# Shifted convolution input: on-chip copies by ScalarE and VectorE, or a trip through device memory

## The chip, the cores and the metric

The kernel runs on one core of a Trainium2 chip. The metric is the device time of one execution in microseconds (us). Before the change the median of 3 runs is 1649.34 us (1648.95 to 1651.52).

## What is computed

One inference step of a small decoder trunk with two layers, for a prompt of 512 tokens and for 8 sample sequences of 4 tokens with a paged cache, in fp32, with a model width of 1024. The first layer has a Conformer convolution module, the second an attention with stick-breaking weights; each is followed by an MLP. The change concerns the prompt's convolution module:

```python
def conformer_conv(h, conv_prev, pw1_w, pw1_b, dw_w, dw_b, ln_g, ln_b, pw2_w):
    a, g = jnp.split(h @ pw1_w + pw1_b, 2, axis=-1)
    u = a * jax.nn.sigmoid(g)
    full = jnp.concatenate([conv_prev, u], axis=1)
    y = lax.conv_general_dilated(full, dw_w[:, None, :], (1,), 'VALID',
                                 dimension_numbers=('NWC', 'WIO', 'NWC'),
                                 feature_group_count=D_MODEL) + dw_b
    y = jax.nn.silu(layer_norm(y, ln_g, ln_b))
    return y @ pw2_w, full[:, -(CONV_WIDTH - 1):]
```

The convolution works on each of the 1024 channels alone, with 31 taps along the tokens. For the prompt `conv_prev` is zero.

## The kernel before

The prompt's activations lie as 8 tiles of 128 channels x 512 tokens. A matrix product in fp32 accuracy is made of three products of fp32r operands, split into a high and a low part (`mm3`, line 326): a weight tile `whi` is cast by ScalarE (line 316), its remainder `wlo` made by VectorE (line 319).

**The projection** (loop from line 783) makes `u` tile by tile, `kt` = 0 to 7, from two weight tiles each. The gate `sg` is an activation on ScalarE (line 866), `u` itself one instruction on VectorE (line 875). The last 30 tokens of `u` are kept in `utail` (line 882). Between these, the sample's own projection and convolution (`sample_pw1`, `sconv`) and the first adaLN matrices of the sample stream (`early`, `ada_group`) are put; `ada_sb` (line 250) is ScalarE's copy of such a result and `adat_B` its transpose on TensorE (line 254).

**The convolution.** Tiles 0 and 2 (`TAPS`) are convolved on VectorE, one instruction for each tap (`conv_taps`, line 690). The six others (`REST`) go to TensorE. There, four copies of 32 channels stand in the four quarters of the partitions, each shifted by one token more than the last, so that one product with a 32-row block of weights adds up four taps: `raw[k][32 j + c, g, t] = u[32 g + c, t + j - 30]`, zero where the token is negative. To make this, `u` is stored to the DRAM tensor `ud` (line 877), whose edges are zeroed once from `zpad` (lines 879 to 881), and read back four times, once for each shift (`conv_load`, lines 700 to 703). All of these transfers go through the queue of GpSimd (`pdma`). The tile `raw` (named `ur`) has two buffers. Tiles 1 and 3 are loaded in the projection; `conv(k)` (line 705) makes the weights `wk` on VectorE (line 707), does its 64 matmuls `cv` (line 713), adds the bias on ScalarE into `y[k]` (line 715), starts the row norm's statistics, and at its end loads the tile after next (line 718). Both engines' work is in order within its queue.

The rest of the kernel is two generators, `sample()` and `prompt()`, taken in turn by costs written in the code (line 1498). The order of the instructions on every engine is set by a planner that simulates a timeline:

```python
    with _tile.TileContext(nc, schedule_with_timeline_sim=True) as tc:
        yoco_step_kernel(tc, *args)
```

`order(ins, after)` (line 333) keeps one instruction behind another in that order without a wait. The two small loads `bias_p` and `ptab` (lines 893, 894) are issued after the last store of `u`.

Of the kernel before, what the change touches and what calls it, by code (L numbers as in the profile page):

```python
# [8 lines left out]
F32 = mybir.dt.float32  # L9
# [8 lines left out]
P = 128  # L18
D = 1024
KT = 8  # L20
T = 512
# [6 lines left out]
CW = 31  # L28
# [83 lines left out]
def yoco_step_kernel(  # L112
# [9 lines left out]
    nc = tc.nc  # L122
# [3 lines left out]
    vec = nc.vector  # L126
    dma = nc.sync.dma_start
    pdma = nc.gpsimd.dma_start

    def pool(stack, name, side=None, **kw):  # L130
        kw.setdefault("bufs", 1)
        return stack.enter_context(tc.tile_pool(name=name, side=side, **kw))
# [6 lines left out]
    dr = pool(ctx, "dr", space=DRAM)  # L139
    done = set()  # L140

    def pm(name="pm"):
        return ps.tile([P, 512], F32, tag="pm", bufs=3, name=name)
# [13 lines left out]
    def tmp(name="tmp"):  # L157
        return pp.tile([P, 512], F32, tag="tmp", bufs=4, name=name)

    def vtiles():  # L160
        return [pp.tile([P, T], F32, tag="v", bufs=KT, name="v") for _ in range(KT)]
# [3 lines left out]
    pl = pool(p1, "p1", "left")  # L165
# [70 lines left out]
    def pcol(row, kt):  # L236
        return prm[:, row, kt : kt + 1]
# [66 lines left out]
    def wstage(src, k, queue=nc.scalar, after=None):  # L304
# [4 lines left out]
            after.append(ins)  # L309
        return st.rearrange("p (k c) -> p k c", k=k)  # L310

    def wsplit(st, c0, cw, wp=wp, after=None, chain=None):
        k = st.shape[1]
        hi = wp.tile([P, k, cw], F32R, tag="whi", bufs=2, name="whi")
        lo = wp.tile([P, k, cw], F32R, tag="wlo", bufs=2, name="wlo")
        ins = nc.scalar.copy(hi, st[:, :, c0 : c0 + cw])  # L316
        if after:
            order(ins, after)
        ins = vec.tensor_tensor(lo, st[:, :, c0 : c0 + cw], hi.bitcast(F32), op=ALU.subtract)  # L319
        if chain is not None:  # L320
            in_turn(chain, ins)
        return hi, lo
# [3 lines left out]
    def mm3(out, whi, wlo, xh, xl, start, stop, after=None):  # L326
        first = mm(out, whi, xh, start=start, stop=False)  # L327
        if after:
            order(first, after)
        mm(out, wlo, xh, start=False, stop=False)  # L330
        latest[:] = [mm(out, whi, xl, start=False, stop=stop)]  # L331

    def order(ins, after):
        tc.add_manual_dep(ins.ins, after.ins.name,
                          mybir.DependencyInfo(mybir.DependencyClass.NoSync, mybir.DependencyReason.DATA), reason="issue order")
        return ins
# [73 lines left out]
    def parts(halves):  # L410
        return (slice(0, 256), slice(256, 512)) if halves else (ALL,)

    def in_turn(chain, ins):
        if chain:
            order(ins, chain[-1])
        chain.append(ins)
# [250 lines left out]
    p0.close()  # L667

    utail = pl.tile([P, KT, CW + 1], F32, name="utail")
    zpad = pl.tile([P, KT, CW + 1], F32, name="zpad")  # L670
    ud = dr.tile([KT, P, T + 32], F32, name="ud")

    s1 = ExitStack()
    sl = pool(s1, "s1", "right")
# [2 lines left out]
    y = vtiles()  # L677
    cnrm = Norm()
    raw = {}


    TAPS = (0, 2)
    REST = [k for k in range(KT) if k not in TAPS]
# [12 lines left out]
    def some_taps(n):  # L696
        for _ in itertools.islice(taps, n):
            pass

    def conv_load(k):  # L700
        raw[k] = pld.tile([P, 4, T + 28], F32, tag="ur", bufs=2, name="ur")
        for j in range(4):
            pdma(raw[k][32 * j : 32 * j + 32], ud[k].rearrange("(g c) t -> c g t", g=4)[:, :, j : j + T + 28])

    def conv(k):
        wk = pld.tile([P, 32, 32], F32, tag="wk", bufs=2, name="wk")
        vec.tensor_tensor(wk, sel4.unsqueeze(1).to_broadcast([P, 32, 32]),
                          wtap[:, k, :].unsqueeze(2).to_broadcast([P, 32, 32]), op=ALU.mult)
        for ts in parts(H_CV and k == KT - 1):
            a = pm("cv")[:, 0 : ts.stop - ts.start]  # L710
            for m in range(8):
                for g in range(4):
                    mm(a[32 * g : 32 * g + 32, :], wk[:, 8 * g + m, :], raw[k][:, g, 4 * m + ts.start : 4 * m + ts.stop],  # L713
                       start=(m == 0), stop=(m == 7), tile_position=(0, 32 * g))
            act(y[k][:, ts], a, AF.Identity, bias=pcol(R_DWB, k))
            cnrm.add(y[k], k, ts)
        if k in REST[:-2]:
            conv_load(REST[REST.index(k) + 2])

    sy = sfm("sy", "sv", 2)  # L720

# [61 lines left out]
    for c in range(4):  # L783
        st = []
        for o in range(2):
            src = conv_pw1_w[0, :, o * D + c * 256 : o * D + c * 256 + 256]
# [13 lines left out]
        if c == 0:  # L800
# [5 lines left out]
            def weights(i, o, after):  # L806
                ws[2 * i + o] = wsplit(st[o], i * P, P, plc if i else wp, after, first_chain)
# [33 lines left out]
            for k in range(KT):  # L841
                t = tmp("ax0")
                nc.scalar.mul(t, ubuf[k], ALPHA)
                axd_dma = pdma(axd[0][k], t)
# [9 lines left out]
        for i in range(2):  # L854
            kt = 2 * c + i
            if c:
                ws = [wsplit(st[o], i * P, P) for o in range(2)]
                accs = [pm("pw1") for _ in range(2)]
                for a, (whi, wlo) in zip(accs, ws):
                    for k in range(KT):  # L860
                        mm3(a, whi[:, k, :], wlo[:, k, :], hhi[k], hlo[k], k == 0, k == KT - 1)
                acc = accs
            else:
                acc = accs[2 * i : 2 * i + 2]
            sg = tmp("sg")
            act(sg, acc[1], AF.Sigmoid, bias=pcol(R_PWB + 1, kt))
            for _ in itertools.islice(early, EIN if c else 0):
                pass
            if kt in TAPS:
                upad[kt] = pld.tile([P, T + CW], F32, tag="upad", bufs=len(TAPS), name="upad")  # L870
                vec.memset(upad[kt][:, 0 : CW - 1], 0.0)
                u = upad[kt][:, CW - 1 : T + CW - 1]
            else:
                u = tmp("u")
            vec.scalar_tensor_tensor(u, acc[0], pcol(R_PWB, kt), sg, op0=ALU.add, op1=ALU.mult)
            if kt not in TAPS:
                u_dma = pdma(ud[kt][:, CW - 1 : T + CW - 1], u)
            if kt == 0:
                pad = order(nc.gpsimd.memset(zpad, 0.0), axd_dma)
                pdma(ud[:, :, 0 : CW - 1].rearrange("k p t -> p k t"), zpad[:, :, 0 : CW - 1])  # L880
                pdma(ud[:, :, T + CW - 1 :].rearrange("k p t -> p k t"), zpad[:, :, 0:2])
            nc.scalar.copy(utail[:, kt, 0 : CW - 1], u[:, T - CW + 1 : T])
            if kt in REST[:2]:
                conv_load(kt)
            some_taps(5)


# [1 line left out]
    bias_p = base.tile([P, 2 * H], F32, name="bias_p")  # L889
    bq = base.tile([P, 8], F32, name="bq")  # L890
    nbq = base.tile([P, 2], F32, name="nbq")
    with tc.issue_after(u_dma.ins):
        pdma(bias_p[:, 0:H], attn_bias.to_broadcast([P, H]))
        pdma(ptab.rearrange("p s g -> p (s g)"), page_table.rearrange("(o s) g -> o (s g)", o=1).to_broadcast([P, NS * NPG]))
    nc.gpsimd.tensor_scalar_mul(bias_p[:, H:], bias_p[:, 0:H], -1.0)
# [646 lines left out]
```

## Time and profile before

| | |
|---|---|
| runs (median, lowest, highest) | 1649.34, 1648.95, 1651.52 us |
| the profiled execution, its own time | 1650.69 us |
| its span, first to last instruction | 1648.9 us |
| busy: TensorE, VectorE, ScalarE, GpSimd | 1553.3, 954.8, 569.4, 181.2 us |
| mean granted clock of TensorE | 0.979 |
| mean DMA rate | 248 GB/s |

The engines are named PE (TensorE matmul), PEld (its weight loads), DVE (VectorE), ACT (ScalarE), POOL (GpSimd) and SP (SyncE); a q behind the name is the engine's sequencer. Times are us from the start of the span. "idle before" is the time that the engine sat idle just before an instruction, with what ended it. The clock is the granted share of TensorE's full speed. `L713` is line 713 of the kernel.

### The profile page before, as it was taken

How to read it: one execution, taken by the hardware profiler on the slowest of the kernel's cores; microseconds unless marked ns; L12 is line 12 of the kernel's file. 1: busy time of each engine (PE TensorE's matmuls, PEld its weight loads, DVE VectorE, ACT ScalarE, POOL GpSimd, SP SyncE). 2: the span in 40 equal slices, each digit the busy share in tenths (PEclk: the TensorE clock that was granted, in tenths of full speed). 3: DMA queues.
4: the chain of work that ended last, by engine and by line, in shares of the span. 5: the costliest groups of instructions: out<-in, count | busy, mean ns of one | idle time of the engine just before them, and what ended most of it. 6: DMA issues, size and time to landing. Idle time of an engine off the chain costs nothing.

```text
span 1648.9 us, 25461 instructions
## 1 busy us (share of the span) xinstructions
PE 1553.3 (94%) x10489; PEld 1088.2 (66%) x10489; DVE 954.8 (58%) x1818; ACT 569.4 (35%) x907; POOL 181.2 (11%) x201
## 2 busy tenths in 40 slices
PE   6999989989999999999899999889889999999995
PEld 4666325656777777777478775557767767566885
DVE  4599545565676655655643448984765434233446
ACT  2322123261332233323332535852362323223342
POOL 1210200000012121110012113021111100000002
PEclk9999999999999999999999999999999999999998
DMA  9898879688667776676889878265546585885311
GB/s 327 279 329 305 230 283 368 246 325 309 225 232 266 272 270 239 224 253 226 343 282 331 281 272 313 96 241 193 193 154 239 185 335 182 352 339 180 96 62 51
DMA packets 152358, 409.24 MB, mean 248 GB/s; under 512 B 8197, under 2 KB 82213, under 8 KB 127651
## 3 DMA queue, kind: packets, MB, share of 16 engines
q1 hardware_dynamic: 50819, 161.86, 26.3%
q0 software_dynamic: 22944, 149.07, 25.2%
q10 hardware_dynamic: 78480, 96.70, 17.6%
q8 instruction: 82, 1.34, 0.3%
q14 instruction: 33, 0.27, 0.0%
HBM read 390.56 MB, written 17.88 MB: 248 GB/s over the span
## 4 chain that ended last, share of the span: by engine, by line
PE 78%; DMA 8%; issue 6%; DVE 5%; ACT 2%; POOL 1%; DVEq 0%; SPq 0%; POOLq 0%; ACTq 0%
PE pd L327 18%; PE pd L331 18%; PE pd L330 17%; PE zt L1071 3%; PE av L1122 3%; PE sd_acc L551 3%; PE cv L713 2%; DMA adaw<-in_ada_w_dram 2%; PE w_acc L578 1%; DMA kraw<-in_cache_k_dram,krow 1%; PE pw L327 1%; PE pw L330 1%; PE pw L331 1%; DMA stage<-in_conv_pw_w_dram 1%; PE ada_A L246 1%
## 5 line engine op out<-in xcount | busy, mean ns | idle before, releaser
L319 DVE TENSOR_TENSOR wlo<-stage,whi 128x1024 fp32r<-128x1024 f32 x184 | 223.1, 1215 | 216.8 <-ACT whi L316 216.4
L327 PE MATMUL pd<-xhi,whi 128*128 128x512 f32 (+1 forms) x832 | 321.4, 388 | 9.6 <-ACT whi L316 5.2
L316 ACT CAST whi<-stage 128x1024 fp32r<-128x1024 f32 x184 | 191.6, 1046 | 400.3 <-PE pd L331 350.6
L330 PE MATMUL pd<-xhi,wlo 128*128 128x512 f32 (+1 forms) x832 | 318.5, 384 | 2.7 <-DVE wlo L319 2.7
L331 PE MATMUL pd<-xlo,whi 128*128 128x512 f32 (+1 forms) x832 | 313.1, 386 | 5.6 <-DVE xlo L460 5.6
L1065 DVE STREAM_TRANSPOSE kt<-kraw 128x512 f32<-128x512 f32 x256 | 164.1, 685 | 138.8 <-DMA kraw<-in_cache_k_dram,krow 92.5
L327 PE MATMUL pd<-h2h,whi 128*128 128x512 f32 (+1 forms) x544 | 206.7, 388 | 1.6 <-DVE v L1240 1.0
L330 PE MATMUL pd<-h2h,wlo 128*128 128x512 f32 (+1 forms) x544 | 205.0, 382 | 0.0
L331 PE MATMUL pd<-h2l,whi 128*128 128x512 f32 (+1 forms) x544 | 205.0, 383 | 0.0
L327 PEld LDWEIGHTS pd<-xhi,whi 128*128 128x128 f32 x832 | 160.7, 193 | 59.7 <-issue 13.7
L331 PEld LDWEIGHTS pd<-xlo,whi 128*128 128x128 f32 x832 | 156.5, 192 | 61.1 <-issue 18.2
L330 PEld LDWEIGHTS pd<-xhi,wlo 128*128 128x128 f32 x832 | 160.9, 193 | 42.1 <-issue 10.8
L1240 DVE SCALAR_TENSOR_TENSOR v<-pd,mod_B,v 128x512 f32<-128x512 f32 x120 | 87.8, 745 | 114.1 <-PE pd L331 113.9
L1043 POOL DMA_INDIRECT kraw<-in_cache_k_dram,krow x64 | 66.3, 1035 | 621.1 <-DVE kt L1065 387.9
L327 PEld LDWEIGHTS pd<-h2h,whi 128*128 128x128 f32 x544 | 101.9, 188 | 34.8 <-issue 10.4
L1215 ACT ACTIVATE relu<-pd 128x512 f32<-128x512 f32 (+1 forms) x68 | 38.9, 572 | 239.7 <-PE pd L331 222.3
L331 PEld LDWEIGHTS pd<-h2l,whi 128*128 128x128 f32 x544 | 101.8, 188 | 28.8 <-issue 9.4
L330 PEld LDWEIGHTS pd<-h2h,wlo 128*128 128x128 f32 x544 | 102.2, 188 | 25.0 <-issue 6.7
L1043 POOL DMA_INDIRECT vt<-in_cache_v_dram,vrow x64 | 70.3, 1098 | 273.4 <-PE av L1122 222.9
L1071 PE MATMUL zt<-kt,qb 128*32 128x128 f32 x2048 | 76.8, 279 | 8.2 <-DVE kt L1065 7.7
L1071 PEld LDWEIGHTS zt<-kt,qb 128*32 128x32 f32 x2048 | 52.8, 110 | 33.2 <-issue 16.4
L368 DVE BATCH_NORM_STATS2 bn<-lnT 128x6 f32<-128x128 f32 x160 | 36.5, 284 | 60.0 <-PE lnT L366 59.8
(300 smaller groups left out, 1987.7 us busy)
## 6 DMA issues: line engine op xcount, KB each, us to landing
sw<-in_mlp_w_dram SPq DMA_DIRECT2D x64, 1024.0 KB
stage<-in_mlp_w_dram ACTq DMA_DIRECT2D x64, 1024.0 KB
adaw<-in_ada_w_dram SPq DMA_DIRECT2D x40, 1024.0 KB
stage<-in_conv_pw_w_dram ACTq DMA_DIRECT2D x10, 1024.0 KB
adaw<-in_ada_w_dram SPq DMA_DIRECT2D x16, 512.0 KB
swkv<-in_w_kv_dram SPq DMA_DIRECT2D x8, 1024.0 KB
stage<-in_w_kv_dram ACTq DMA_DIRECT2D x8, 1024.0 KB
ur<-ud POOLq DMA_DIRECT2D x24, 270.0 KB, 8.0
```

What stands on the lines that cost most here:

```text
L316: ins = nc.scalar.copy(hi, st[:, :, c0 : c0 + cw])
L319: ins = vec.tensor_tensor(lo, st[:, :, c0 : c0 + cw], hi.bitcast(F32), op=ALU.subtract)
L327: first = mm(out, whi, xh, start=start, stop=False)
L330: mm(out, wlo, xh, start=False, stop=False)
L331: latest[:] = [mm(out, whi, xl, start=False, stop=stop)]
L551: mm(acc[32 * g : 32 * g + 32, :], hT[:, kk * 2 + kp, :], blk[:, kp * D + c * 512 : kp * D + c * 512 + 512], start=(kk == 0), stop=(kk == ...
L1043: nc.gpsimd.indirect_dma_start(out=out, out_offset=None, in_=cache.rearrange("g (r e) h d -> (g r) (e h d)", e=2), in_offset=bass.Indirect ...
L1065: ins = vec.transpose(kt[:, 2 * x : 2 * x + 2, :], raw[x].rearrange("p (e c) -> p e c", e=2)[:, :, c0 : c0 + 256])
L1071: behind(mm(zt[u][32 * g : 32 * g + 32, f * P : f * P + P], qb[:, u, hh * 8 + bl].rearrange("p x q -> p (x q)"), kt[:, :, bl * 32 : bl * 3 ...
L1122: behind(mm(av[32 * g : 32 * g + 32, :], wT[u][:, i, e, a, :], vt[:, e * D + u * 512 : e * D + u * 512 + 512], start=(a == 0 and i == 0), ...
L1215: latest_act[:] = [act(r, a, AF.Relu)]
L1240: ins = vec.scalar_tensor_tensor(v[kt][:, ts], a, gt[:, kt, 8:9], v[kt][:, ts], op0=ALU.mult, op1=ALU.add)
```

## The change

`u` of the six `REST` tiles is written into `y[k]` directly. The store to `ud`, the zeroing and the four reads go. `conv_load` clears the edges of `raw` (two memsets on VectorE) and copies 16 blocks of 32 partitions x some 512 tokens, each from one quarter of the partitions into another or the same. For tiles 1 and 3, in the projection, all 16 are on ScalarE, put into the loop five at a time; for the four tiles that are loaded within the convolutions, 8 are on ScalarE and 8 on VectorE. ScalarE's copies are ordered behind the last `whi` cast issued so far. `bias_p` and `ptab` are issued after an earlier transfer.

```diff
+    last_whi = []
+
     def wsplit(st, c0, cw, wp=wp, after=None, chain=None):
...
         ins = nc.scalar.copy(hi, st[:, :, c0 : c0 + cw])
         if after:
             order(ins, after)
+        last_whi[:] = [ins]
...
     utail = pl.tile([P, KT, CW + 1], F32, name="utail")
-    zpad = pl.tile([P, KT, CW + 1], F32, name="zpad")
-    ud = dr.tile([KT, P, T + 32], F32, name="ud")
...
     raw = {}
+    loads = []
...
-    def conv_load(k):
+    def conv_load(k, both):
         raw[k] = pld.tile([P, 4, T + 28], F32, tag="ur", bufs=2, name="ur")
-        for j in range(4):
-            pdma(raw[k][32 * j : 32 * j + 32], ud[k].rearrange("(g c) t -> c g t", g=4)[:, :, j : j + T + 28])
+
+        vec.memset(raw[k][:, :, 0 : CW - 1], 0.0)
+        vec.memset(raw[k][:, :, T + CW - 4 :], 0.0)
+        for g in range(4):
+            for j in range(4):
+                out = raw[k][32 * j : 32 * j + 32, g, CW - 1 - j : min(T + CW - 1 - j, T + 28)]
+                src = y[k][32 * g : 32 * g + 32, 0 : out.shape[-1]]
+                if both and (g + j) % 2:
+                    vec.tensor_copy(out, src)
+                else:
+                    order(nc.scalar.copy(out, src), last_whi[0])
+                    yield
...
         if k in REST[:-2]:
-            conv_load(REST[REST.index(k) + 2])
+            for _ in conv_load(REST[REST.index(k) + 2], True):
+                pass
...
             else:
-                u = tmp("u")
+                u = y[kt]
             vec.scalar_tensor_tensor(u, acc[0], pcol(R_PWB, kt), sg, op0=ALU.add, op1=ALU.mult)
-            if kt not in TAPS:
-                u_dma = pdma(ud[kt][:, CW - 1 : T + CW - 1], u)
-            if kt == 0:
-                pad = order(nc.gpsimd.memset(zpad, 0.0), axd_dma)
-                pdma(ud[:, :, 0 : CW - 1].rearrange("k p t -> p k t"), zpad[:, :, 0 : CW - 1])
-                pdma(ud[:, :, T + CW - 1 :].rearrange("k p t -> p k t"), zpad[:, :, 0:2])
             nc.scalar.copy(utail[:, kt, 0 : CW - 1], u[:, T - CW + 1 : T])
             if kt in REST[:2]:
-                conv_load(kt)
+                loads.append(conv_load(kt, False))
+            for _ in itertools.islice(itertools.chain(*loads), 5 if kt < KT - 1 else 32):
+                pass
             some_taps(5)
...
-    with tc.issue_after(u_dma.ins):
+    with tc.issue_after(axd_dma.ins):
```

## Rows read from the trace of the kernel before

**Rows 1.** The page's first part: busy time, share and instructions of each engine.

```profile
PE 1553.3 (94%) x10489; PEld 1088.2 (66%) x10489; DVE 954.8 (58%) x1818; ACT 569.4 (35%) x907; POOL 181.2 (11%) x201
```

**Rows 2.** Busy time by stretch: us, each engine (instructions), granted clock, DMA share, GB/s.

```profile
65.00:155.00 90.00, 86.54 (x533) 59.26 (x531) 87.42 (x156) 25.23 (x46) 11.44 (x20) 1.00 0.88 294
155.00:248.00 93.00, 83.10 (x643) 31.64 (x635) 49.68 (x148) 17.73 (x30) 10.71 (x20) 0.97 0.82 272
248.00:1649.00 1401.00, 1335.28 (x9061) 965.60 (x9061) 795.04 (x1465) 507.21 (x805) 151.71 (x144) 0.98 0.66 240
85.00:106.00 21.00, 17.62 (x116) 10.64 (x112) 21.00 (x34) 3.93 (x6) 0.56 (x1) 1.00 1.03 345
196.00:208.00 12.00, 7.04 (x58) 2.29 (x54) 6.61 (x23) 1.10 (x2) 3.23 (x6) 0.98 1.01 257
208.00:220.00 12.00, 12.00 (x96) 3.76 (x100) 3.11 (x12) 0.69 (x1) 0.00 (x0) 0.88 0.16 33
```

**Rows 3.** TensorE's waits, 65 to 155 us, then 155 to 250: total, times, longest.

```profile
PE ada_B L246 <- DMA adaw<-in_ada_w_dram: 3.4, 3, 2.2
...
PE cv L713 <- DMA ur<-ud: 5.0, 1, 5.0
PE w_acc L578 <- DMA sw<-in_mlp_w_dram: 3.7, 4, 1.4
```

**Rows 4.** TensorE in order of time around 208 us: start, us, instruction, idle before.

```profile
207.94 5.12 PE L713 MATMUL cv<-ur,wk 128*32 128x512 f32 x32 [4.96 <-DMA ur<-ud]
...
213.57 3.64 PE L713 MATMUL cv<-ur,wk 128*32 128x512 f32 x32
```

**Rows 5.** GpSimd's issues of the reads; the page's DMA issues (KB each, landing).

```profile
81.08 2.19 POOL L703 DMA_DIRECT2D ur<-ud  x4 [5.29 <-DMA ud<-u]
...
194.87 2.18 POOL L703 DMA_DIRECT2D ur<-ud  x4 [11.04 <-PE cv L713]
...
ur<-ud POOLq DMA_DIRECT2D x24, 270.0 KB, 8.0
```

**Rows 6.** TensorE in order of time, the first and last wait for `adaw`.

```profile
98.82 1.06 PE L246 MATMUL ada_B<-adaw,cT 128*32 128x512 f32 x8 [0.20 <-DMA adaw<-in_ada_w_dram]
...
105.85 1.07 PE L246 MATMUL ada_B<-adaw,cT 128*32 128x512 f32 x8 [0.96 <-DMA adaw<-in_ada_w_dram]
```

**Rows 7.** VectorE, then TensorE, in order of time in the projection.

```profile
113.77 1.23 DVE L319 TENSOR_TENSOR wlo<-stage,whi 128x1024 fp32r<-128x1024 f32 x1 [0.81 <-ACT whi L316]
...
122.49 1.21 DVE L319 TENSOR_TENSOR wlo<-stage,whi 128x1024 fp32r<-128x1024 f32 x1
...
124.48 0.39 PE L330 MATMUL pw<-xhi,wlo 128*128 128x512 f32 x1
...
135.37 0.60 PE L254 MATMUL adat_B<-c,ada_sb 128*128 128x128 f32 x4
```

**Rows 8.** Groups of instructions: busy us, mean ns, idle before.

```profile
L1278 ACT CAST xhi<-v 128x512 fp32r<-128x512 f32 x8 | 4.8, 604 | 0.0
...
L715 ACT ACTIVATE v<-cv,prm 128x512 f32<-128x512 f32 x6 | 4.1, 685 | 36.8 <-PE cv L713 36.8
...
L946 DVE COPY qr<-qr 32x1024 f32<-32x1024 f32 x3 | 2.1, 685 | 0.1
...
L980 DVE COPY nka<-kv_sb 32x256 f32<-32x256 f32 x4 | 1.1, 286 | 0.1
...
L707 DVE TENSOR_TENSOR wk<-c,wtap 128x1024 f32<-128x1024 f32 x6 | 7.3, 1220 | 3.8 <-PE cv L713 3.8
```

**Rows 9.** ScalarE in order of time.

```profile
133.99 0.22 ACT L882 COPY utail<-u 128x30 f32<-128x30 f32 x1 [2.46 <-DVE u L875]
134.56 0.59 ACT L250 COPY ada_sb<-ada_B 128x512 f32<-128x512 f32 x1 [0.36 <-DVE sy L745]
135.39 1.05 ACT L316 CAST whi<-stage 128x1024 fp32r<-128x1024 f32 x1 [0.24 <-PE pw L331]
...
181.41 0.42 ACT L910 ACTIVATE shT<-sy 128x256 f32<-128x256 f32 x1 [7.45 <-DVE sy L909]
```

## The prediction, made before the changed kernel ran

> **What bounds the kernel now.** I first read the page's head: TensorE is busy for 94% of the span [rows 1], so time is won only where TensorE waits, and a saving elsewhere is hidden. Next came busy time by stage [rows 2]. The change touches two stages. In the projection (65 to 155 us) TensorE idles 90.00 - 86.54 = 3.5 us, VectorE is busy 87.42 of 90 us, and ScalarE 25.23. In the convolution (155 to 248 us) TensorE idles 93.00 - 83.10 = 9.9 us, with VectorE at 49.68 and ScalarE at 17.73. The waits then name what ended that idle time [rows 3]: 3.4 us are weights `adaw` still on the DMA, in the projection; in the convolution 5.0 us are one wait of `cv` for `ur`, the transfer that the change removes, and 3.7 us are sample weights; the rest is smaller.
>
> The order of time shows that one wait [rows 4]: TensorE starts a convolution at 207.94 us after 4.96 us of waiting, since 203.0. Its four reads were issued at 194.87 [rows 5], when the DMA engines were full (share 1.01 between 196 and 208 us, [rows 2]), and the last landed some 11 us after its issue ended at 197.05, against a median of 8.0. After it the clock is low: 32 matmuls take 5.12 us, the next 32 take 3.64 [rows 4]; between 208 and 220 us the granted clock is 0.88 of the upper level, in the projection it is 1.00 [rows 2].
>
> **The change, part by part.** The sum is made against the profiled execution, 1650.69 us, whose span is 1648.9; the median of the runs shown, 1649.34, is 1.35 us below it. A measurement of this kernel can tell about 0.2%, 3.3 us, from no change.
>
> *Removed: the wait for `ur`.* The four tiles loaded inside the convolutions no longer come by DMA. Gain 5.0 us [rows 3]. With the pause goes the slow clock behind it: 5.12 - 3.64 = 1.5 us [rows 4]. Next in line to be late are the copies themselves, priced below.
>
> *Removed: traffic.* Six stores of 256 KB, 24 reads of 270 KB and 128 KB of zeros go, about 8.3 MB. In the projection, the reads of tile 1, issued at 81.08 [rows 5], compete with the `adaw` blocks that TensorE awaits three times, first at 98.8 and last at 105.9 us [rows 6]. They are 1.1 MB; at the 345 GB/s of that stretch [rows 2] they delay the rest by 3.2 us. But VectorE is busy 21.00 of 21 us there [rows 2]. The low half of a later weight tile, `wlo`, is made at 122.49 and is ready at 123.70, and TensorE wants it at 124.48 [rows 7], 0.8 us of slack; VectorE idles another 0.8 us before the preceding `wlo` [rows 7]. A TensorE that arrives 3.2 us earlier therefore keeps about 1.6 us and waits for VectorE with the rest. I take 1.6; the bounds are 0 and 3.4. By the Trainium skill, DMA: Bandwidth & Descriptors, Queues, rings and completion order, each DMA engine goes round the queues that have work, a packet at a time, so that a queue taken away hands its turns to the others at once. By that rule the `adaw` wait would go whole and its term be 3.4; no row here shows the turns. This is a rival below.
>
> *Added: ScalarE's copies.* 32 for the first two tiles in the projection, then 8 for each of four tiles, 64 in all. No row shows one of 32 partitions; the nearest, a ScalarE cast of 128x512 between on-chip tiles, takes 604 ns [rows 8], and I take it. The lower end is `utail`'s 30 columns at 0.22 us [rows 9], the upper end 685 ns, the eviction of 128x512 with a bias [rows 8]. In the projection five copies follow each `utail` copy, 3.0 us, on an engine that idles 65 of 90 us [rows 2], and TensorE's waits there name `adaw` alone [rows 3], so the weight casts have slack. The tightest place is 133.99: `ada_sb` follows at 134.56 and a `whi` cast at 135.39 [rows 9]. If `ada_sb` falls behind the copies, TensorE's `adat_B` at 135.37 [rows 7] waits about 2.6 us: 133.99 + 0.22 + 3.0 + 0.59 less 135.37 is 2.4, and 0.2 for the handover. The program issues `ada_sb` first, so I take 0 and keep 2.6 as an end.
>
> *Added: VectorE's copies.* 8 for each of four tiles, 32 in all. The nearest rows are copies between partition quarters: 32x256 in 286 ns and 32x1024 in 685 [rows 8], so 512 columns take 286 + 256 x 399/768 = 419 ns; the ends are those two rows. That is 3.4 us a tile, 13.4 in all. The two memsets of a tile, 120 columns and 4, I put at 0.3 us together, what the copy of 256 columns takes [rows 8].
>
> *What covers them.* Tile k+2 is copied after convolution k ends, while convolution k+1 runs: 64 matmuls, two times 3.64 us [rows 4], 7.2 us. On ScalarE the copies are 8 x 0.604 behind the eviction (0.69), 5.5 us; on VectorE 3.4 + 0.3 behind the 1.2 us of `wk`, 4.9 us [rows 8]. Both are below 7.2, so I cost them at 0. Without that cover a tile costs up to 5.5 us of TensorE wait. What queues behind them on VectorE is the sample's layer norm, whose `shT` ScalarE makes at 181.41 after 7.45 us of waiting [rows 9], and the statistics of the row norm.
>
> *Moved.* The queue of GpSimd loses 32 issues, and the two small loads for `bias_p` and `ptab` no longer stand behind the last store; VectorE's work on them can come earlier. The sample weights' 3.7 us [rows 3] lie beside the prompt's norm and I give them 0. The other uses of GpSimd are untouched.
>
> Sum: 5.0 + 1.5 + 1.6 = 8.1 us less, so 1650.69 - 8.1 = 1642.6 for the profiled execution, and 1641.2 for the median. I say **1641**. From 248 us on TensorE is busy 1335 of 1401 us [rows 2], so an earlier start should carry through to the end.
>
> **The rivals.**
> *All of the traffic's wait goes* (the rule above). For it: `adaw` landed late while the engines were over 1.0 [rows 2]. Against it: VectorE is full there. The sum is then 5.0 + 1.5 + 3.4 = 9.9, giving 1639.4 us.
> *The copies take the place of the transfer.* The next tile is late by as much as before, because a copy stands in an in-order queue behind other work (`wk`, the rsqrt chain, `ssq`). For it: both queues serve the sample too. Against it: 5.5 us against 7.2. Only the 1.6 stays: 1647.7 us. With `ada_sb` late as well and nothing won, it would be 1652. In this case the trade happens without effect.
> *VectorE's copies land on the path, slower.* Each group of 8 stands at the head of VectorE's queue just when convolution k ends, and the sample's norm (and so `sd_acc` and `w_acc` on TensorE, whose order is fixed) waits behind it. All 13.4 us on the path, less the 8.1 won, is 5.3 slower: 1654.6 us. It decides from the point where over 8.1/13.4 = 60% of the copying is waited for. For it: the chain to `shT` is already VectorE-bound. Against it: VectorE idles 43 us of that stage [rows 2].
> *The planner.* The instruction order of every engine comes from a planner's simulated run (line 1538), so a new early order could shift later meetings of the two streams, among the 1401.00 - 1335.28 = 66 us that TensorE idles after 248 us [rows 2]. It can go either way and widens the range.
>
> **How the numbers follow.** Forecast 0.52, all of the traffic's wait 0.20: both faster, 0.72. Copies in place of the transfer 0.14: same. VectorE on the path 0.14: slower. The low end, 1634, is all the TensorE idle time of both stages (3.5 + 9.9) and the clock's 1.5 off the median. The high end, 1652, is the median with nothing won and 2.6 us of late `ada_sb`. Beyond it lies most of the slower case, and little else.
>
> **What would show it.** Right: no wait of `cv` on anything over 1 us, 64 matmuls of a convolution in about 7.2 us throughout, granted clock 1.00 up to 230 us, the first `pd` matmul some 8 us before 247.9, and `adaw` waits under 3.4. The copies should read near 0.60 and 0.42 us. Wrong: `cv` waiting for ScalarE or VectorE at `ur`, `adat_B` waiting for `ada_sb`, `wlo` ending TensorE's idle time in the projection, or an unchanged early gain that is lost again after 250 us.

## The result and the profile after

The changed kernel takes **1658.75 us** (median of 5 runs, 1656.23 to 1663.75) against 1649.34 before: ratio 1.0055, 95% interval 1.0032 to 1.0078. It is slower by 0.55%, some 9 us, where 8 us less were forecast. The profiled execution took 1656.23 us with a span of 1654.5, 5.6 us over the span before; it is the fastest of its runs, so its trace shows the smaller part of the loss. Every ratio below is to runs of the kernel before that were made beside it, and these had medians from 1647.62 to 1652.94 us; so ratios can be compared, single times only roughly.

The page's first part, after:

```profile
PE 1553.6 (94%) x10489; PEld 1087.2 (66%) x10489; DVE 969.1 (59%) x1862; ACT 608.6 (37%) x971; POOL 160.4 (10%) x168
```

Against [rows 1] TensorE's work is the same, VectorE gained 14.3 us and ScalarE 39.2, about what the copies cost (below). So the time lies in when things run, not in how much. Busy time by stretch, with the columns of [rows 2]:

```profile
65.00:155.00 90.00, 88.26 (x529) 60.01 (x528) 80.25 (x161) 43.34 (x76) 3.46 (x7) 0.98 0.78 278
155.00:248.00 93.00, 85.66 (x609) 35.92 (x607) 79.27 (x201) 46.10 (x75) 1.14 (x2) 0.94 0.38 143
...
170.00:208.00 38.00, 38.00 (x316) 11.83 (x312) 36.55 (x94) 22.87 (x38) 0.00 (x0) 1.00 0.09 29
320.00:360.00 40.00, 26.10 (x155) 12.07 (x154) 19.68 (x84) 11.15 (x25) 0.00 (x0) 0.70 0.72 273
...
220.00:231.00 11.00, 6.02 (x29) 4.73 (x32) 8.90 (x48) 2.60 (x6) 0.00 (x0) 0.68 0.19 82
```

The last three stretches of the kernel before:

```profile
170.00:208.00 38.00, 32.98 (x286) 11.23 (x282) 19.20 (x68) 4.47 (x8) 9.11 (x17) 0.99 0.90 247
320.00:360.00 40.00, 32.70 (x213) 21.74 (x213) 33.11 (x120) 24.47 (x49) 0.00 (x0) 0.91 0.71 270
...
220.00:231.00 11.00, 11.00 (x108) 3.69 (x100) 0.89 (x4) 0.21 (x1) 0.00 (x0) 1.00 0.94 373
```

Four things are to be seen. TensorE idles 1.7 us in the projection instead of 3.5. It is busy without a gap from 170 to 208 us, where it had idled 5.0. But in that stretch VectorE is busy 36.55 of 38 us instead of 19.20, and the DMA engines all but stop: 29 GB/s instead of 247, in part because the reads are gone. And TensorE is then dry twice: 5.0 us between 220 and 231, with the clock at 0.68, and 13.9 us between 320 and 360 instead of 7.3, at 0.70 instead of 0.91.

TensorE's waits after, 65 to 155 and 320 to 360 us (us in total, times, longest):

```profile
PE us L786 <- ACT pw1sb L781: 1.7, 2, 1.6
...
PE sd_acc L554 <- DMA sw<-in_mlp_w_dram: 5.2, 4, 2.3
PE smp L518 <- DVE sred L516: 5.0, 2, 3.3
```

The waits of [rows 3] for `adaw` (3.4 us) and for `ur` (5.0) are gone. No convolution waits for a copy. The new ones at 320 us are all of the sample stream: its weights and its norm. (One more, `mrb` with 3.0 us, was there before with 3.3.)

TensorE in order of time, after, with the columns of [rows 4]:

```profile
209.36 3.64 PE L554 MATMUL sd_acc<-sw,shT 128*32 128x512 f32 x32
...
223.54 0.41 PE L518 MATMUL smp<-sred,meanm 128*128 128x32 f32 x2 [1.68 <-DVE sred L516]
...
228.87 2.05 PE L389 MATMUL rb<-dg,onesm 128*128 128x128 f32 x8 [2.38 <-DVE dg L388]
230.84 5.33 PE L581 MATMUL w_acc<-sw,hT 128*32 128x512 f32 x32
...
238.77 0.50 PE L330 MATMUL pd<-xhi,whi 128*128 128x512 f32 x1
```

and before:

```profile
184.41 4.00 PE L551 MATMUL sd_acc<-sw,shT 128*32 128x512 f32 x31
...
218.62 3.62 PE L578 MATMUL w_acc<-sw,hT 128*32 128x512 f32 x32
```

The prompt's first `pd` comes at 238.77 us, 9.2 us ahead of the 247.92 of before. The sample's second product `sd_acc` comes 25 us late, and `w_acc`, its MLP whose weights are the largest stream of the queue of SyncE, 12 us late. Before, `w_acc` began between the matmuls of the last convolution; now it begins when the convolutions are over and TensorE has run dry.

VectorE in order of time, after, shows why `shT` is late:

```profile
174.73 0.75 DVE L692 SCALAR_TENSOR_TENSOR v<-upad,prm,v 128x512 f32<-128x512 f32 x1
175.51 3.51 DVE L712 COPY ur<-v 32x512 f32<-32x512 f32 x8
179.05 0.19 DVE L434 TENSOR_SCALAR ve<-smp 128x32 f32<-128x32 f32 x1
...
183.26 0.18 DVE L440 TENSOR_TENSOR rw<-rw,vh 128x32 f32<-128x32 f32 x1
183.37 1.22 DVE L719 TENSOR_TENSOR wk<-c,wtap 128x1024 f32<-128x1024 f32 x1
184.60 3.49 DVE L712 COPY ur<-v 32x511 f32<-32x511 f32 x8
188.13 0.75 DVE L692 SCALAR_TENSOR_TENSOR v<-upad,prm,v 128x512 f32<-128x512 f32 x1
188.79 0.19 DVE L441 SCALAR_TENSOR_TENSOR rs<-rw,rs 128x32 f32<-128x32 f32 x1
...
200.94 0.36 DVE L522 TENSOR_TENSOR sy<-sy,rs 128x256 f32<-128x256 f32 x1
...
208.27 0.41 DVE L920 TENSOR_TENSOR shT<-shT,sy 128x256 f32<-128x256 f32 x1
```

and the same chain before:

```profile
176.04 0.19 DVE L431 TENSOR_SCALAR ve<-smp 128x32 f32<-128x32 f32 x1
...
180.03 0.43 DVE L519 TENSOR_TENSOR sy<-sy,rs 128x256 f32<-128x256 f32 x1
...
181.86 0.42 DVE L911 TENSOR_TENSOR shT<-shT,sy 128x256 f32<-128x256 f32 x1 [0.48 <-ACT shT L910]
```

From `ve` to `sy` the chain took 4.0 us; now it takes 21.9. Each small step of 0.19 us waits its turn behind a group of copies (3.5 us) or a tap (0.75 us). The copies were expected there. The taps (L692) were not: before, all 60 ran ahead of the convolutions, the last at 163.8 us; now 20 lie in this stretch. ScalarE, after, tells how they came there:

```profile
154.18 1.25 ACT L714 COPY ur<-v 32x512 f32<-32x512 f32 x2
155.44 0.82 ACT L690 ACTIVATE v<-upad,prm 128x512 f32<-128x512 f32 x1
```

Line 690 is the first tap of tile 2, an activation on ScalarE that its other 30 taps on VectorE need. Before it ran at 86.59 us. The planner, which had pulled it forward, now keeps it behind ScalarE's copies, 69 us later.

SyncE's queue, which loads the sample's weights, waits for the consequence (150 to 260 us, first the kernel after, then before):

```profile
SPq L579 <- PE sd_acc L554: 57.4, 3, 56.5
```

```profile
SPq L576 <- PE sd_acc L551: 31.2, 4, 29.9
```

The load of the next weights waits for a buffer that `sd_acc` holds. That is one half of the DMA pause of 170 to 208 us; the other half are the reads that the change removes. Of the 9.40 MB that the kernel before moved there, the queues of GpSimd (q0) and of SyncE (q1) carried (packets, MB, share of 16 engines):

```profile
q0 software_dynamic: 1205, 4.11, 52.1%
q1 hardware_dynamic: 576, 4.19, 29.5%
```

After, neither carries anything there.

### The profile page after: what moved, and what is told of

It is laid out like the page before. It is cut to its first block, busy times and chain, and to the rows that moved or that the text cites. A ratio compares the mean times of both kernels' runs of the same rounds, so it can differ in the third digit from the quotient of the medians.

```text
span 1654.5 us, 25507 instructions
## 1 busy us (share of the span) xinstructions
PE 1553.6 (94%) x10489; PEld 1087.2 (66%) x10489; DVE 969.1 (59%) x1862; ACT 608.6 (37%) x971; POOL 160.4 (10%) x168
## 4 chain that ended last, share of the span: by engine, by line
PE 83%; DMA 5%; DVE 5%; issue 4%; ACT 2%; POOL 0%; DVEq 0%; ACTq 0%; POOLq 0%; SPq 0%
PE pd L330 18%; PE pd L334 18%; PE pd L333 18%; PE zt L1080 4%; PE av L1131 3%; PE cv L725 3%; PE sd_acc L554 2%; PE w_acc L581 2%; PE pw L330 2%; PE pw L333 2%; PE pw L334 2%; DMA stage<-in_conv_pw_w_dram 1%; DMA adaw<-in_ada_w_dram 1%; PE ada_A L246 1%; PE lnT L369 1%
## 5 line engine op out<-in xcount | busy, mean ns | idle before, releaser
L330 PE MATMUL pd<-xhi,whi 128*128 128x512 f32 (+1 forms) x832 | 317.8, 384 | 9.6 <-ACT whi L318 5.7
L1131 PE MATMUL av<-vt,wT 128*32 128x512 f32 x512 | 63.3, 598 | 2.1 <-DMA vt<-in_cache_v_dram,vrow 2.1
```

The lines of the kernel that those rows point to most:

```text
L1131: behind(mm(av[32 * g : 32 * g + 32, :], wT[u][:, i, e, a, :], vt[:, e * D + u * 512 : e * D + u * 512 + 512], start=(a == 0 and i == 0), ...
```

## The experiments

**Theory A**: VectorE's order delays the sample's norm, and with it the sample's `sd_acc` and `w_acc`; the prompt's early lead is only sample work put off, paid back at 320 us on a dry TensorE. **Theory B**: the delay early is harmless, and the planner's other order later on costs the time. "Shift" below is the start of the prompt's matmuls (`pd`, `zt`, `av`) less that of the same ones before, each from one trace: the median over the 50 us that begin at the time named; for the change it is -12.1 us at 300 us and +7.3 at 350.

**No copies.**

```diff
...
-        for g in range(4):
+        for g in range(0):
```

> Leaves out the 96 copies (the convolution reads tiles that are zeroed once), so what TensorE, the transfers and the order can reach without them is seen. Theory A (the time is lost because the copies and the late taps hold the sample's norm on VectorE, so shT comes at about 208 us, the sample's weights stop on the DMA from 170 to 208 us, and TensorE runs dry at 325 to 355 us): shT at 180 to 185 us, DMA share above 0.5 from 170 to 208 us, no dry stretch at 325 to 355, total 1636 to 1644 us. Theory B (the planner's order after 300 us loses the time by itself, whatever the early stage does): shT early as well, but the total stays at 1654 to 1662 us. Theory C (the engine time of the copies is what costs, 14 us on VectorE and 39 on ScalarE): like A.

1645.61 us, ratio 0.9967 (0.9951 to 0.9983), just above theory A's range and far below theory B's. `w_acc` at 217.6 us, shift -6.8. Without copies the removal of the transfers pays 0.3%. The taps still ran late (19 after 165 us), yet `shT` was made at 189.4: taps alone do not do it.

**Tile 2's first tap ahead of the copies.** The activation of line 690 is issued right behind that tile's `utail` copy.

```diff
-        act(y[k], up[:, 0:T], AF.Identity, scale=prm[:, R_DW, k : k + 1], bias=pcol(R_DWB, k))
...
             nc.scalar.copy(utail[:, kt, 0 : CW - 1], u[:, T - CW + 1 : T])
+            if kt in TAPS:
+                act(y[kt], upad[kt][:, 0:T], AF.Identity, scale=prm[:, R_DW, kt : kt + 1], bias=pcol(R_DWB, kt))
```

> Only the activation that starts tile 2's taps is moved: it is issued right behind tile 2's utail copy, ahead of the copies, so that the 30 taps of tile 2 are ready from about 90 us instead of 156. All copies stay. Theory A, in the form that the late taps are the larger part: no tap after 170 us, shT between 185 and 198 us, total 1644 to 1652 us. Theory A, in the form that VectorE's copies are the larger part: shT still past 200 us, total 1654 to 1660. Theory B: no change, 1656 to 1660.

1653.69 us, ratio 1.0020 (1.0005 to 1.0035) against the change's 1.0055; the two intervals overlap a little, and theory A's 1644 to 1652 us was missed. The trace is clearer: no tap after 165 us, `w_acc` at 218.5, shift -3.1 instead of +7.3. Busy time of the stretch in question, VectorE at 28.99 us and the DMA at 153 GB/s:

```profile
170.00:208.00 38.00, 38.00 (x322) 12.84 (x326) 28.99 (x86) 23.86 (x39) 0.00 (x0) 1.00 0.41 153
```

All copies are still there, so 0.35% of the loss is not their price but the company they keep. That is the smaller part of the 0.88% between the change and its kernel without copies: the other 0.53% (1.0020 against 0.9967) stays with `shT` as early as without copies (188.5 against 189.4).

**All copies on ScalarE.**

```diff
-                if both and (g + j) % 2:
+                if False:
```

> All 16 copies of every tile go to ScalarE, none to VectorE; the late taps stay. Theory A, taps the larger part: shT at 195 to 205 us, total 1652 to 1658 us. Theory A, VectorE's copies the larger part: shT below 192 us and total 1644 to 1650. Theory D (copies on the path of the convolution): 16 x 0.616 + 0.69 = 10.5 us on ScalarE against 7.2 us of matmuls, so cv waits about 3 us for each of four tiles and the total is 1660 us or more.

1657.58 us, ratio 1.0047 (1.0029 to 1.0065). `shT` came 8 us earlier than in the change, at 200.4, but `w_acc` at 232.6; shift +7.9. VectorE's 13.4 us of copies moved away change nothing that can be told. The taps stay late, and 16 copies a tile on ScalarE (9.9 us) exceed a convolution's 7.1 us; which of the two matters more, this run does not show. One of TensorE's waits, 65 to 250 us:

```profile
PE cv L725 <- ACT ur L714: 2.9, 3, 1.5
```

**The taps alone late, in the kernel before.**

```diff
-            some_taps(5)
+            some_taps(5 if kt < 6 else 0)
```

> The kernel before, with its DMA loads, but the taps of tile 2 are issued in the convolution stage instead of the projection. Theory A: the taps fill the gaps between the small steps of the sample's norm; shT some 5 to 12 us later than 181 us, total 1650 to 1656 us. If late taps alone do nothing: shT within 2 us of 181, total 1648 to 1651 us.

1650.5 us, ratio 1.0000 (0.9983 to 1.0017). `shT` 5.7 us later, at 187.6, `w_acc` at 223.1, shift -0.3. With 30 taps in the stage and no copies, nothing is lost.

**The change, with the taps held behind `shT`.**

```diff
-            some_taps(5)
+            some_taps(5 if kt < 6 else 0)
...
-            vec.scalar_tensor_tensor(y[k], up[:, j : j + T], prm[:, R_DW + j, k : k + 1], y[k], op0=ALU.mult, op1=ALU.add)
+            ins = vec.scalar_tensor_tensor(y[k], up[:, j : j + T], prm[:, R_DW + j, k : k + 1], y[k], op0=ALU.mult, op1=ALU.add)
+            if k:
+                order(ins, norm_end[0])
```

> The changed kernel with all its copies, on both engines; the 30 taps of tile 2 are issued in the convolution stage and kept, on VectorE, behind the last step of the sample's norm (shT). So the taps are as late as in the change or later, but no longer between the norm's steps. Theory A (what matters is when shT is ready, not where the taps or copies run): shT at 185 to 193 us, no dry stretch at 320 to 360 us (TensorE idle there under 9 us, against 13.9), total 1646 to 1654 us. Theory B (the planner's order after 300 us): idle 12 us or more there and 1656 us or more. If late taps cost by themselves: the row norm waits for tile 2, first pd matmul after 245 us.

1655.22 us, ratio 1.0039 (1.0018 to 1.0059). `shT` was early, at 189.0, TensorE idled 9.1 us between 320 and 360 us instead of 13.9, and the time was still lost: theory A as first put falls here. VectorE in order of time, and one of TensorE's waits (65 to 250 us), show what is missing:

```profile
218.74 0.18 DVE L435 TENSOR_SCALAR ve<-smp 128x32 f32<-128x32 f32 x1
218.86 0.75 DVE L693 SCALAR_TENSOR_TENSOR v<-upad,prm,v 128x512 f32<-128x512 f32 x1
...
228.10 0.43 DVE L523 TENSOR_TENSOR sv<-sv,rs 128x256 f32<-128x256 f32 x1
```

```profile
PE lnT L370 <- DVE v L693: 4.6, 1, 4.6
```

The taps now held the sample's second norm, which stands between `sd_acc` and `w_acc` (230.9 us). But the prompt's row norm (`lnT`) waited for the last tap too, and the first `pd` came at 248.69: the last of the three expectations came true as well, and this run cannot tell a late `w_acc` from a late row norm. From here on theory A reads (A'): what counts is when `w_acc` starts, not `shT`; the runs that bear on it are the next ones.

**The norm alone late, in the kernel before.** 40 passes of ScalarE over `sy`, which change nothing in it, delay `shT`; no copies, the transfers as before.

```diff
+        for _ in range(40):
+            act(sy, sy, AF.Identity)
         act(hT, sy, AF.Sigmoid)
```

> The kernel before, with nothing changed but 40 idle passes of ScalarE over the sample's normed activations (128x256, 0.42 us each, each waiting for the last) ahead of the sigmoid, so shT comes about 17 to 25 us later than 181 us while VectorE, the transfers and the taps are as before. Theory A: the sample's weights stop on the DMA for as long, TensorE idles 12 us or more between 320 and 360 us, and the total rises to 1655 to 1663 us. Theory B or C: within 3 us of the kernel before.

1659.12 us, ratio 1.0061 (1.0040 to 1.0082): the change's loss, without the change. Its busy time by stretch, and SyncE's wait from 150 to 260 us:

```profile
170.00:208.00 38.00, 37.76 (x326) 13.27 (x324) 15.40 (x53) 19.81 (x46) 9.13 (x17) 1.00 0.67 147
320.00:360.00 40.00, 25.57 (x158) 12.28 (x157) 20.02 (x85) 11.19 (x25) 0.00 (x0) 0.74 0.74 280
```

```profile
SPq L576 <- PE sd_acc L551: 51.9, 4, 50.7
```

Even the prompt's lead is there (-10.7 us at 300) and its reversal (+8.2 at 350). TensorE is dry at 320 us as after the change: busy 25.57 of 40 us against 26.10. Of the 147 GB/s, 4.50 of 5.60 MB are the reads in GpSimd's queue; SyncE's moved nothing, as after the change. So that lead needs neither copies nor missing transfers; it is sample work put off. With half the dose (20 passes):

> The half dose of the delay: the kernel before with 20 idle passes of ScalarE instead of 40. Theory A': shT at about 190 to 194 us and w_acc at 219 to 225; since shT at 188 cost nothing with late taps, the delay is mostly covered and the total is 0 to 4 us above the kernel before, against 10 to 11 for the full dose. If the cost is simply in proportion to the delay: 5 to 6 us above.

1661.98 us, ratio 1.0051 (1.0034 to 1.0068). `w_acc` at 225.2, shift at 350 us +3.4, between 0 and +8.2 as a dose would have it. The end did not follow in proportion: 0.51% is 8.4 us, where A' expected 0 to 4 and a loss in proportion 5 to 6; the trace loses another 7.5 us after 350 us, which this theory doesn't explain.

**VectorE's copies on GpSimd**, on top of the early tap; then also half of the first two tiles' copies there.

```diff
-                    vec.tensor_copy(out, src)
+                    nc.gpsimd.tensor_copy(out, src)
```

> As the run with tile 2's activation moved ahead, but the 32 copies that were VectorE's are GpSimd's, which has nothing to do in this stage. No row shows such a copy; the nearest, GpSimd's two-input operation on 128x512, takes 1.28 us, so one copy is taken at 0.6 to 1.3 us and eight at 5 to 10, against 7.2 us of matmuls. Theory A: shT at 180 to 186 us, total 1643 to 1650 us if a copy is under 0.9 us. If it is over, cv waits for GpSimd up to 3 us for each of four tiles and the total is 1650 to 1658.

> As the last, and GpSimd takes 8 of the 16 copies of the first two tiles as well, so that ScalarE has 48 copies instead of 64. If ScalarE's copies in the projection cost nothing, as was forecast: within 2 us of the last run. If they delay the weight casts: 2 to 5 us less.

1660.94 us, ratio 1.0075 (1.0056 to 1.0094), and 1665.49 us, 1.0109 (1.0087 to 1.0131). The copies on GpSimd in the first, all of line 711:

```profile
L711 POOL COPY ur<-v x32: 602/608/1507, 174.4 to 218.4; 32x512 f32<-32x512 f32 x16, 32x511 f32<-32x511 f32 x8, 32x510 f32<-32x510 f32 x8
```

(ns, least, median, most). Both miss their expectations: a copy stayed under 0.9 us (median 608 ns) and the total was not 1643 to 1650, and the second is 4.5 us above the first, not within 2 or below. In the first, VectorE was free and `shT` early (188.3), but the last convolution ended at 249.6 us instead of 219.5 with the early tap alone. Here the convolutions themselves are late: TensorE idled 4.7 us before `sd_acc` and 3.6 before `w_acc` with no cause that the profile names, and `w_acc`, begun at 221.4, stood ahead of nearly two convolutions. Why, stays open.

**A third buffer in the kernel before**, loaded three convolutions ahead.

```diff
-        raw[k] = pld.tile([P, 4, T + 28], F32, tag="ur", bufs=2, name="ur")
+        raw[k] = pld.tile([P, 4, T + 28], F32, tag="ur", bufs=3, name="ur")
...
-        if k in REST[:-2]:
-            conv_load(REST[REST.index(k) + 2])
+        if k in REST[:-3]:
+            conv_load(REST[REST.index(k) + 3])
...
-            if kt in REST[:2]:
+            if kt in REST[:3]:
```

> The kernel before, DMA loads and all, with a third buffer for ur: three tiles are loaded in the projection and each later one three convolutions ahead, so that no convolution waits for its transfer. Theory A' (the total follows the start of the sample's first MLP product w_acc, from which 32 MB of sample weights must still stream): the 5.0 us wait and the slow clock behind it go, w_acc starts at 211 to 214 us instead of 218.6, total 4 to 8 us under the kernel before in the same call. If the wait for ur is hidden anyway: within 2 us of it.

**1646.66 us, ratio 0.9951 (0.9936 to 0.9965)**: faster than both kernels, with the transfers kept. No convolution waits any more; what grew is the wait in the projection, where the third tile's reads now lie (TensorE's waits, 65 to 250 us):

```profile
PE ada_B L246 <- DMA adaw<-in_ada_w_dram: 5.0, 3, 3.1
```

`w_acc` came at 215.9, shift -4.9. The 5 us that the change went for were to be had without touching VectorE's queue.

**The late tiles moved on chip by DMA**, 16 transfers each, half from GpSimd's and half from ScalarE's queue, with the early tap.

```diff
-                if both and (g + j) % 2:
-                    vec.tensor_copy(out, src)
+                if both:
+                    (pdma if (g + j) % 2 else nc.scalar.dma_start)(out, src)
```

> As the run with tile 2's activation moved ahead; the first two tiles are still copied by ScalarE, but the blocks of the four later tiles are moved by the DMA engines straight from y[k] into ur, 16 transfers of 32 partitions each, 8 issued by GpSimd and 8 by ScalarE. No store, no read from device memory, no copy on VectorE. Theory A': shT at 180 to 186 us; if 16 transfers take under 8 us from issue to landing, no cv wait and the total is 1 to 6 us under the kernel before; if their issue (8 x 0.55 on GpSimd) and landing exceed the 7.2 us of a convolution, cv waits 2 to 4 us each time and the total is 3 to 10 us above.

1654.13 us, ratio 1.0002 (0.9989 to 1.0016): no gain. ScalarE's evictions come late on an engine that issues half of the transfers (at 196.43 us eight issues held its queue for 15.69 us), and the row norm waits (TensorE's waits, 65 to 250 us):

```profile
PE lnT L369 <- ACT v L726: 8.2, 1, 8.2
```

**Which of the copies costs?** With the early tap, first no copies for the four later tiles (the 32 of the projection stay), then ScalarE's half of them, then VectorE's half. In the last two:

```diff
+        if both:
+            raw[k] = raw[REST[REST.index(k) - 2]]
...
-                    vec.tensor_copy(out, src)
+                    pass
```

(the half of VectorE kept: `elif not both` in place of `else`).

> As the run with tile 2's activation moved ahead, without the 64 copies of the four later tiles (those convolutions read the first two tiles' data again); ScalarE's 32 copies in the projection stay. It splits what the copies cost besides the taps. If the later copies cost it: total as without any copies, 5 to 7 us under the kernel before. If ScalarE's copies in the projection cost it: within 2 us of the run with all copies and the early activation, 1 to 4 us above the kernel before.

> The kernel with tile 2's first tap activation ahead of the copies (ratio 1.0020), less VectorE's 32 copies of the four later tiles: ScalarE's 32 stay. The kernel leaves those 32 out and writes the others into the two tiles that the first loads use, so its convolutions read partly old data. If VectorE's copies carry the rest of the loss: near 0.9963, with shT no later than 188 us and the first w_acc near 219. If ScalarE's carry it: near 1.0020. If both in proportion: near 0.999. If the order after 350 us decides and no copy does: any of these, with the shift of the prompt at 350 us unchanged at about -3 us.

> The same kernel less ScalarE's 32 copies of the four later tiles: VectorE's 32 stay, and the 32 others are left out. If VectorE's copies carry the rest of the loss: near 1.0020. If ScalarE's carry it: near 0.9963. If both in proportion: near 0.999. If the order after 350 us decides: any of these, with the shift of the prompt at 350 us at about -3 us.

Ratios 0.9963 (0.9948 to 0.9978), 1.0007 (0.9991 to 1.0022) and 1.0018 (1.0006 to 1.0031), beside 1.0020 with all copies. The 32 copies of the projection cost nothing: 0.9963 is as good as no copies at all (0.9967). For the later ones neither engine's half stands out. And at 350 us the four kernels lie within 2.8 us, with shifts of -3.7, -0.9, -2.4 and -3.1 us in this order; the three with late copies lose 2.7 to 3.5 us more by the end of their traces, the first wins 2.8. What separates them falls after 350 us, where no copy runs. That part stays open.

**Copies a convolution earlier**, with a third buffer and the early tap: three tiles copied in the projection.

> The kernel with tile 2's first tap activation ahead of the copies, with a third buffer for the shifted input: three tiles are copied by ScalarE in the projection (48 copies) and three by ScalarE and VectorE within the convolutions, each one convolution earlier than before, 24 copies on VectorE in place of 32. If what is left of the loss is the meeting of VectorE's copies with the sample's norm: a quarter of them goes, the first w_acc comes near 217 us and the ratio is 0.998 to 1.001. If the copies' deadline costs it: no wait of cv or of the row norm for a copy, and 0.996 to 0.998. If the order after 350 us decides: about 1.002 with the prompt at 350 us some 3 us ahead of the kernel before.

1657.71 us, ratio 1.0038 (1.0024 to 1.0052): a miss for all three expectations, and a demonstration. With no late tap at all, `w_acc` is late again, at 229.0 us, and the shift +6.0. ScalarE, then VectorE, in order of time:

```profile
174.31 5.00 ACT L713 COPY ur<-v 32x512 f32<-32x512 f32 x8
179.34 0.42 ACT L514 ACTIVATE ssq<-sy 128x256 f32<-128x256 f32 x1
```

```profile
184.69 3.44 DVE L711 COPY ur<-v 32x512 f32<-32x512 f32 x8
188.17 0.19 DVE L434 TENSOR_SCALAR ve<-smp 128x32 f32<-128x32 f32 x1
```

The norm's sum of squares (`ssq`) stands behind ScalarE's first group of copies, and its next step (`ve`) behind VectorE's second. With the early tap alone the norm slipped in ahead of the first group. So copies alone are enough to hold the norm; which of them it meets is a matter of a few us of placement.

**All together.** Start of the first `w_acc` and the prompt's shift at 350 us, from the traces, in order of the first; beside them the ratio of the runs:

```
                               w_acc at   shift    ratio
before, third buffer              215.9    -4.9   0.9951
no copies                         217.6    -6.8   0.9967
early tap                         218.5    -3.1   1.0020
before                            218.6     0.0   1
projection copies only            219.1    -3.7   0.9963
late copies, VectorE's half       219.3    -2.4   1.0018
late copies, ScalarE's half       221.7    -0.9   1.0007
before, taps late                 223.1    -0.3   1.0000
before, norm late by half         225.2    +3.4   1.0051
direct DMA                        225.4    +4.7   1.0002
early tap, third buffer           229.0    +6.0   1.0038
the change                        230.8    +7.3   1.0055
taps behind shT                   230.9    +6.0   1.0039
before, norm late                 231.7    +8.2   1.0061
copies on ScalarE alone           232.6    +7.9   1.0047
```

Up to 223.1 us nothing is lost against before; from 225.2 on all seven kernels are late, with and without copies. The ratios follow in the main: six of the seven lose 0.38 to 0.61%, but direct DMA loses nothing, and the early tap and VectorE's half lose 0.2% with an early `w_acc`. The two with GpSimd, whose convolutions end late, stand outside the list. Theory B is not needed for the first 350 us, and the kernel before with its norm alone delayed speaks against it; for what comes after 350 us nothing here excludes it, since single traces gain or lose up to 7.5 us there. Nor did any run give the sample's weights another buffer, so the pause of that stream and the late start of `w_acc` are not told apart.

## Why the prediction was wrong

**Right.** The `ur` wait (5.0 us) went, and the low clock behind it: the granted clock was 1.00 from 170 to 208 us, and a convolution's 64 matmuls took 7.07 us. (From 220 to 231 us, where the forecast asked for 1.00 too, it was 0.68.) The `adaw` wait went whole, as the Trainium skill, DMA: Bandwidth & Descriptors, Queues, rings and completion order, would have it; the turns of the queues themselves no run shows. TensorE's idle time in the projection fell by 1.7 us only, because a wait for `pw1sb` is new. That this comes near the 1.6 of the forecast is luck: the wait lies at 69.51 us, 29 us ahead of the first `adaw` block and ahead of the first copy (76.6), and the kernel without copies has it too (1.6 us). VectorE's `wlo`, which the forecast named as the next one late, ended no wait in this trace; with the early tap it did. TensorE in order of time after the change, and its wait with the early tap (65 to 155 us):

```profile
69.51 0.63 PE L786 MATMUL us<-c,pw1sb 128*128 128x32 f32 x4 [1.57 <-ACT pw1sb L781]
...
194.69 7.07 PE L725 MATMUL cv<-ur,wk 128*32 128x512 f32 x64
```

```profile
PE pw L333 <- DVE wlo L322: 2.5, 2, 1.7
```

The first `pd` was 9.2 us ahead where some 8 were asked for. `adat_B` did not wait for `ada_sb`. The gain of 8.1 us by itself was at the edge of what the runs bear out: without any copies the kernel won 0.33%, 5.4 us (2.8 to 8.1 by the interval).

**The copies' sizes were right, and so was their cover against the convolution.** All of line 714 and of line 712 (ns, least, median, most):

```profile
L714 ACT COPY ur<-v x64: 613/616/622, 76.6 to 205.5; 32x512 f32<-32x512 f32 x32, 32x510 f32<-32x510 f32 x16, 32x511 f32<-32x511 f32 x16
```

```profile
L712 DVE COPY ur<-v x32: 414/418/423, 175.5 to 206.7; 32x512 f32<-32x512 f32 x16, 32x511 f32<-32x511 f32 x8, 32x510 f32<-32x510 f32 x8
```

616 and 418 ns against 604 and 419. The memsets took 0.22 us a tile against 0.3.

**The step that failed** is "Both are below 7.2, so I cost them at 0". The cover of a convolution covers the convolution. The next sentence of the prediction named what queues behind the copies, the sample's norm with `shT`, and then priced it at nothing in the sum. Its delay was 26 us, and the measured time is 9 us above the kernel before where 8 below were forecast. The norm's delay alone, in the kernel before, costs 0.61%; taking the late taps from the change gives back 0.35%. What the late copies cost besides, 0.53%, no run explains. The mechanism was the rival on VectorE, `sd_acc` and `w_acc` late in a fixed order, given a chance of 0.14 and 1654.6 us. That rival's price was sized wrongly too: it counted 13.4 us of copying, where 20 taps of 0.75 us came on top, and it asked how much of the copying was waited for, where up to 350 us the loss goes with the start of `w_acc`. The argument against it, that VectorE idles 43 us of that stage, was an average: those 43 us did not lie between the steps of a chain that must pass a queue in order.

**Two more steps missed.** The planner was expected to move meetings after 248 us; it moved an activation of the projection by 69 us, and with it 20 taps. And "an earlier start should carry through to the end" took the lead at `pd` for a gain; the delayed norm alone, with the transfers in place, shows the same lead. The prediction's own last sign of failure, an early gain that is lost again after 250 us, is what the trace shows: -12.1 us at 300, +7.3 at 350, +5.6 at the end. The high end of 1652 left the slower case out.

## What to carry to other kernels

Work that is hidden behind one engine's matmuls is not hidden from its own queue: before costing it at nothing, list the dependent chains that pass that queue in the same stretch, and follow each to what it lets start, here a weight stream of another part of the program. A lead of one stream is a gain only if the other has not fallen behind; compare both streams' landmarks. And when one transfer lands late, try an earlier load first: a third buffer won 0.49% where taking the transfer away lost 0.55%.

## What the chip showed that was not expected

A copy of 32 partitions costs ScalarE as much as a whole tile: 616 ns for 32x512, beside 604 for a cast of 128x512 [rows 8]; so 16 such copies cost 9.9 us, more than a convolution's 7.1. GpSimd's copy of the same shape took 608 ns, no more than ScalarE's, but up to 1507. And the granted clock was low in two stretches that waits had thinned out: 0.68 where TensorE was busy 6.02 of 11 us, 0.70 where it was busy 26.10 of 40, with 1.00 in the full stretch from 170 to 208 us. Before, it was 0.98 in the stretch with the wait (196 to 208 us) and 0.88 in the full one behind it [rows 2]. So work behind a wait can take longer too, and the lost time is more than the idle time that the waits list: 32 matmuls of `w_acc` took 5.33 us after, where the granted clock was 0.68, and 3.62 before, where it was 1.00.
